# Another written order of the steps in a hybrid attention and gMLP block

## The chip, the cores and the metric

The kernel runs on one core of a Trainium2 chip. The metric is the device time of one execution in microseconds. Engines are named as in the profile: PE is TensorE (matrix products), PEld its weight loads, DVE is VectorE, ACT is ScalarE, POOL is GpSimd, and SP is the queue that issues most transfers.

## The reference

One encoder block on x of 1024 tokens by 1024 channels. One input projection feeds an attention branch, a gated spatial branch, and merge gates:

```python
h = rmsnorm(x, norm_gain)
z = jnp.einsum('bsd,de->bse', h, w_in)
q, k, v, gate_a, u_in, v_in, gate_b, g_merge = jnp.split(z, IN_SPLITS, axis=-1)
q = axial_rope(rmsnorm(q by head, q_gain), ...)      # 8 heads of 64
k = axial_rope(rmsnorm(k by head, k_gain), ...)      # 2 heads of 64
attn = block_attention(q, k, v) * jax.nn.silu(gate_a)
y_a = attn @ w_proj_attn
u = jax.nn.gelu(u_in)
vv = layernorm(jax.nn.gelu(v_in), ln_v_gain, ln_v_bias)
v_mix = jnp.einsum('gij,bcjgd->bcigd', w_spatial, vv) + b_spatial   # within chunks of 128 tokens
gm = u * v_mix * jax.nn.silu(gate_b)
y_b = gm @ w_proj_gmlp
g = jax.nn.sigmoid(g_merge + b_merge)
y = g[0] * y_a + g[1] * y_b
return rmsnorm(x + y @ w_out, final_gain)
```

## The kernel before

Nearly every matrix product is done as three products of a high and a low part (lines 184 to 187, and likewise elsewhere), so each operand is cast by ScalarE (the high part, line 124 or 286) and subtracted by VectorE (the low part, line 130 or 287). The stages follow each other:

- The k and v projections (tile kv, lines 203 to 227) run over eight slices of 128 channels of x. Each slice is loaded, split into a tile xhl, and used for 48 products. The eight xhl tiles fill the eight buffers of tag "X".
- v_group(0) to v_group(3) (line 458) compute the spatial branch's v input, 48 products each, from the xhl tiles and from weights in tiles nh and nl; the two nl tiles fill the two buffers of tag "ptr". A GELU on ScalarE (line 465) writes each result to a vst tile. v_post (line 368) is the layer norm of one 128-token chunk, and spatial (line 381) mixes positions.
- load_pair, norm_part and norm_split (lines 291 to 315) load x again in four pairs of channel slices (tiles xp), multiply by the rows' norm rB (line 299), and split into f16 tiles x16. The pairs and the two vst tiles share the four buffers of tag "qT". The x16 tiles of slices 4 to 7 lie in tag "X".
- prep_q (line 505) loads, casts and splits one eighth of the q weights. Its raw tile comes from the four buffers "wraw", which also hold the two raw halves of the spatial weights (load_wsp, line 474) until bias_term (line 493) has read them. Its output lies in "ptr".
- q_group (line 529) makes q for 256 tokens, q_norm (425) its head norm and rotary positions, q_split (431) its split and transposes. head_norm and rope (395 and 410) do the same for k (tile kn), split and k_transposes follow.
- The maximum of v (lines 1032 to 1038: the multiplication by the rows' norm, and a reduction to vab) gives a scale for v; lines 1082 to 1097 finish it, beginning with a transpose vabT on TensorE, and vS holds the scaled and split v.
- scores (line 629) handles 128 queries of one head: products, maximum (637), exponential (641), split (647 and 648), and a transposing transfer to a tile T (652). mix2 (654) multiplies T with v for two blocks. run_fill (685) is half of one tile of the u, a or b projections, whose weights come from prep_next; all of them use one PSUM bank, tag "z". v_affine (559) applies the layer norm's gain and bias after the spatial product.
- proj_b, x_chunk, pair_weights, gate, proj_a and square_out (lines 701 to 994) are the output side: projections, merge gates and the preparation of the output weights. The output product and the final norm end the kernel.

From line 998 on, one flat list of calls sets the written order of all this. The compiler doesn't keep it: it forecasts when each instruction is ready, places instructions on the engines by that, and lets the written order decide between those that are ready. A few blocks under tc.high_priority() go ahead of all. Once placed, each engine and each transfer queue executes strictly in its order and waits for the buffers and values that the head of its queue needs. The scales of the weights come from squares (line 334), whose raw tiles are loaded from ScalarE's queue into tag "xa" (line 333).

## Time and profile before

| | |
|---|---|
| three runs | 714.37, 715.13, 716.05 us; median 715.13 |
| the profiled execution | 716.34 us, of which 714.6 us is its span |
| PE, DVE, ACT, POOL busy | 684.1, 576.6, 478.8, 99.8 us |
| instructions | 12246 |
| mean granted clock of TensorE | 0.99 |

In the timelines a row has the start, the busy time, the engine, the line, the operation and its tiles; the brackets hold how long the engine sat idle before it and what it waited for. A row with xN merges N like instructions, and its time then runs from the first one's start to the last one's end. In lists of waits the three figures are the total, the number of times, and the longest.

### The profile page before, as it was taken

Reading aid. Unit: us, or ns where it says so; the run is one execution under the profiler, and the core shown is the slowest. Engines: PE = TensorE matmul, PEld = TensorE weight load, DVE = VectorE, ACT = ScalarE, POOL = GpSimd, SP = SyncE. Lnnn points to the kernel's source line nnn. Section 1 sums busy time; section 2 is a strip of 40 time slices with the busy share of each in tenths; the row PEclk is TensorE's granted clock in tenths of the full one; section 3 lists DMA queues with packets and bytes.
Section 4 is the critical chain, followed back from the end, with each engine's and each line's share of the span. In section 5 each row is a group of like instructions: output and inputs, shape, how many; then the busy total and the mean of one; then the engine's idle time right before and its main releaser. Section 6 shows DMA issues by size and latency. Waiting matters only on the chain.

```text
span 714.6 us, 12246 instructions
## 1 busy us (share of the span) xinstructions
PE 684.1 (96%) x4753; PEld 398.0 (56%) x4753; DVE 576.6 (81%) x831; ACT 478.8 (67%) x890; POOL 99.8 (14%) x114
## 2 busy tenths in 40 slices
PE   8999799998998999999999999999999999999996
PEld 8888545454464555545546885644645564444443
DVE  6577999999898997899788998979879887972233
ACT  6676558976788987789676697585784647831011
POOL 0026043044020011001000022001020102000000
PEclk9999999999999999999999999999999999999998
DMA  8990444634679997799997730440520043410202
GB/s 298 402 403 9 162 156 152 210 59 90 118 167 169 198 202 131 149 223 178 175 187 169 228 104 1 143 152 0 202 78 16 1 165 128 179 53 36 118 30 89
DMA packets 159818, 102.40 MB, mean 143 GB/s; under 512 B 136208, under 2 KB 136848, under 8 KB 159760
## 3 DMA queue, kind: packets, MB, share of 16 engines
q1 hardware_dynamic: 158320, 97.14, 52.8%
q10 hardware_dynamic: 1440, 4.47, 1.6%
q8 instruction: 37, 0.61, 0.3%
q14 instruction: 21, 0.17, 0.1%
HBM read 63.85 MB, written 4.19 MB: 95 GB/s over the span
## 4 chain that ended last, share of the span: by engine, by line
PE 48%; DVE 18%; DMA 12%; ACT 11%; issue 5%; POOL 4%; SPq 1%; POOLq 0%; ACTq 0%; DVEq 0%
PE out L187 4%; PE out L186 4%; PE out L185 4%; DMA T<-p 3%; DVE p L648 3%; DMA wraw<-in_wall_dram 3%; PE g L187 3%; PE g L185 3%; DMA xraw<-in_xT_dram 3%; PE g L186 3%; DVE nm L637 2%; PE o L662 2%; ACT P L641 2%; ACT p L647 2%; DMA xn<-in_x_dram 1%
## 5 line engine op out<-in xcount | busy, mean ns | idle before, releaser
L648 DVE SCALAR_TENSOR_TENSOR p<-P,ri,p 128x1024 f16<-128x1024 f32 x64 | 83.4, 1309 | 12.2 <-ACT p L647 11.8
L641 ACT ACTIVATE P<-s,nm 128x1024 f32<-128x1024 f32 x64 | 71.1, 1111 | 29.0 <-DVE nm L637 18.9
L637 DVE TENSOR_REDUCE nm<-s 128x1 f32<-128x1024 f32 x64 | 77.5, 1215 | 1.9 <-PE s L635 1.8
L647 ACT ACTIVATE p<-P,ri 128x1024 f16<-128x1024 f32 x64 | 72.7, 1140 | 3.6 <-DVE ri L644 1.9
L662 PEld LDWEIGHTS <-vS 128*64 128x64 f16 x1536 | 45.9, 111 | 19.2 <-issue 16.6
L662 PE MATMUL o<-T,vS 128*64 128x128 f16 x1536 | 51.2, 222 | 5.5 <-DMA T<-p 5.4
L634 PE MATMUL s<-kT,qT 128*128 128x512 f16 x128 | 49.2, 384 | 2.2 <-ACT P L641 2.2
L186 PE MATMUL out<-wo,yhl 128*128 128x512 f16 (+2 forms) x136 | 49.5, 366 | 0.0
L187 PE MATMUL out<-wo,yhl 128*128 128x512 f16 (+2 forms) x136 | 49.3, 366 | 0.0
L185 PE MATMUL out<-wo,yhl 128*128 128x512 f16 (+2 forms) x136 | 49.0, 366 | 0.0
L635 PE MATMUL s<-kT,qT 128*128 128x512 f16 x128 | 48.9, 382 | 0.0
L953 ACT ACTIVATE sq<-xr 128x1024 f32<-128x1024 f32 x7 | 7.4, 1059 | 58.8 <-DVE xr L1374 58.4
L1374 DVE SCALAR_TENSOR_TENSOR xr<-out,osc,xr 128x1024 f32<-128x1024 f32 x7 | 9.0, 1284 | 40.7 <-PE out L187 40.7
L185 PE MATMUL g<-x,wg 128*128 128x512 f16 x96 | 36.5, 380 | 0.0
L187 PE MATMUL g<-x,wg 128*128 128x512 f16 x96 | 36.4, 379 | 0.1
L186 PE MATMUL g<-x,wg 128*128 128x512 f16 x96 | 36.4, 379 | 0.0
L279 POOL TENSOR_SCALAR scg<-scg 128x1 f32<-128x1 f32 x8 | 2.0, 250 | 197.7 <-ACT usg L278 197.7
L186 PE MATMUL q<-wq,x 128*128 128x512 f16 x64 | 24.7, 388 | 2.7 <-DVE wq L287 2.7
L185 PE MATMUL q<-wq,x 128*128 128x512 f16 x64 | 24.8, 388 | 0.5 <-ACT wq L286 0.5
L186 PE MATMUL v<-nl,xhl 128*128 128x512 f32 x64 | 25.2, 393 | 0.0
L186 PE MATMUL yb<-gm,wh 128*128 128x512 f32 x64 | 25.2, 393 | 0.0
L185 PE MATMUL v<-nh,xhl 128*128 128x512 f32 x64 | 25.1, 392 | 0.0
(571 smaller groups left out, 1925.9 us busy)
## 6 DMA issues: line engine op xcount, KB each, us to landing
wraw<-in_wall_dram SPq DMA_DIRECT2D x91, 256.0 KB, 3.2
graw<-in_wall_dram SPq DMA_DIRECT2D x16, 512.0 KB, 4.7
xraw<-in_xT_dram SPq DMA_DIRECT2D x13, 512.0 KB, 5.6
xn<-in_x_dram SPq DMA_DIRECT2D x8, 512.0 KB, 8.2
xp<-in_xT_dram SPq DMA_DIRECT2D x8, 512.0 KB, 6.3
wor<-in_wall_dram SPq DMA_DIRECT2D x8, 512.0 KB, 5.2
xr<-in_x_dram SPq DMA_DIRECT2D x8, 512.0 KB, 3.8
out_dram<-xr SPq DMA_DIRECT2D x7, 512.0 KB, 2.6
```

The source lines that it names most:

```text
L185: pe.matmul(o, ah, bh, start=start, stop=False)
L186: pe.matmul(o, ah, bl, start=False, stop=False)
L187: pe.matmul(o, al, bh, start=False, stop=stop)
L634: pe.matmul(sp[:, H(hf)], qs, kT[v][:, 0, H(hf)], start=True, stop=False)
L635: pe.matmul(sp[:, H(hf)], qs, kT[v][:, 1, H(hf)], start=False, stop=True)
L637: dve.tensor_reduce(out=nm, in_=sp, axis=AX.X, op=ALU.max, negate=True)
L641: act.activation(Pt, sp, AF.Exp, bias=nm, accum_out=rsum)
L647: act.activation(hi, Pt, AF.Copy, scale=ri)
L648: dve.scalar_tensor_tensor(out=lo, in0=Pt, scalar=ri, in1=hi, op0=ALU.mult, op1=ALU.subtract)
L662: pe.matmul(ot[64 * h:64 * h + 64, C(k)], vS[:, kt, v, 64 * vl:64 * vl + 64], T[:, h, 8 * p + kt, :], start=(n == 0), stop=(n == len(parts ...
L953: act.activation(sq, xn, AF.Square, accum_out=rs)
L1374: dve.scalar_tensor_tensor(out=xr[tt], in0=sps[tt], scalar=osc[:, 4:5], in1=xr[tt], op0=ALU.mult, op1=ALU.add)
```

## The change

The list of calls is written in another order. No call is added or removed, and no function is changed. In the part up to the scores:

```diff
+    early = scales(["q"] + order[:4], ["xa"] * 8)
+    v_group(0)
     bsp = t2("bsp")
...
     Ak, Bk = (heads(t) for t in tabk)
-    early = scales(["q"] + order[:4], ["xa"] * 8)
-    v_group(0)
+    load_pair(0)
+    rB = t4("rB", "rB")
...
+    v_group(1)
+    load_pair(1)
+    with tc.high_priority():
+        scales_end(*early)
...
     load_wsp(0)
+    load_wsp(1)
+    v_group(2)
+    load_pair(2)
+    prep_q(0)
+    v_post(0)
+    norm_part(3)
+    load_pair(3)
+    norm_part(2)
+    ktmp = t4("vS", "ktmp")
+    head_norm(kn, ktmp, 0, 8, "kf")
+    norm_part(0)
+    prep_q(1)
+    scale_wsp()
+    norm_part(1)
+    prep_q(2)
+    v_group(3)
     v3 = vn.rearrange("p (t e) -> p t e", e=128)
...
-    v_post(0)
-    rB = t4("rB", "rB")
...
-    load_wsp(1)
-    scale_wsp()
-    v_group(1)
-    ktmp = t4("vS", "ktmp")
-    head_norm(kn, ktmp, 0, 8, "kf")
-    load_pair(1)
-    load_pair(0)
-    v_group(2)
...
-    v_post(1)
-    prep_q(0)
-    prep_q(1)
-    load_pair(2)
-    norm_part(4)
-    load_pair(3)
-    rope(kn, ktmp, Ak, Bk, 8, 2)
-    norm_split(4)
-    v_group(3)
-    prep_q(2)
     bias_term(0)
     prep_q(3)
+    v_post(1)
+    norm_part(7)
     prep_q(4)
-    norm_part(1)
+    norm_part(5)
+    norm_part(4)
     prep_q(5)
...
+    rope(kn, ktmp, Ak, Bk, 8, 2)
     v_post(6)
...
+    prep_q(6)
+    norm_split(4)
...
+    spatial(0)
+    norm_split(3)
+    v_post(3)
+    v_post(2)
+    norm_split(0)
+    norm_split(7)
+    prep_q(7)
...
+    k_transposes(0)
+    norm_split(1)
+    norm_split(6)
     k_transposes(1)
+    norm_split(5)
+    norm_split(2)
     k_transposes(2)
+    bias_term(1)
+    q_group(0)
+    q_norm(0)
```

In the attention some thirty calls change places by a few positions: q_norm(2) moves from before the first scores to behind the fifth, q_norm(3) from behind the fifth to behind the seventh, v_affine(0) from behind the twenty-third scores to behind the twelfth, and mix2, run_fill, prep_next and scores are interleaved differently. In the output side:

```diff
+    x_chunk(0)
...
     load_chunk(1)
-    pws[0] = pair_weights(0)
-    x_chunk(0)
     proj_b(0)
+    load_chunk(2)
     proj_b(1)
     proj_b(2)
+    pws[0] = pair_weights(0)
     proj_b(3)
+    proj_b(4)
+    load_chunk(3)
+    proj_b(5)
     x_chunk(1)
-    load_chunk(2)
-    proj_b(4)
     x_chunk(2)
-    load_chunk(3)
     x_chunk(3)
     make_forms(gat, 2, g_tile, GA, ASUB, AHI, ALO)
-    proj_b(5)
     proj_b(6)
...
-    pws[4] = pair_weights(4)
-    gate(4)
     square_out(4)
     square_out(3)
+    pws[4] = pair_weights(4)
     pws[5] = pair_weights(5)
+    gate(4)
```

## The prediction

> **What bounds the kernel now.** I read the page first, then the busy time by stages, then the waits of TensorE, then the timelines of all queues between 40 and 92 us. The page:

> ```profile
> PE 684.1 (96%) x4753; PEld 398.0 (56%) x4753; DVE 576.6 (81%) x831; ACT 478.8 (67%) x890; POOL 99.8 (14%) x114
> ```

> TensorE is busy for 684.1 of 714.6 us, and no operation is added or removed. So the new order can only win or lose in the remaining 30.5 us, and in stretches at a reduced clock. By stages (columns: length, busy time and instructions of PE, PEld, DVE, ACT, POOL, then clock, DMA share, GB/s):

> ```profile
> 0.00:40.00 40.00, 36.57 (x250) 33.92 (x251) 21.83 (x45) 27.89 (x46) 3.21 (x10) 1.00 0.95 355
> 40.00:81.40 41.40, 41.29 (x237) 34.27 (x236) 35.49 (x54) 26.86 (x47) 14.81 (x13) 1.00 0.49 188
> 81.40:90.50 9.10, 3.81 (x17) 1.37 (x16) 9.10 (x13) 5.79 (x8) 0.00 (x0) 0.96 0.26 86
> 90.50:141.40 50.90, 49.33 (x366) 25.09 (x366) 46.41 (x84) 40.99 (x83) 15.76 (x18) 0.97 0.56 176
> 141.40:380.00 238.60, 226.63 (x2209) 121.43 (x2208) 213.68 (x278) 192.02 (x347) 38.22 (x30) 0.99 0.84 155
> 380.00:445.00 65.00, 63.84 (x449) 47.48 (x447) 59.84 (x88) 50.89 (x92) 7.67 (x4) 1.00 0.49 134
> ```

> The densest loss is 81.4 to 90.5, at the start of the q projection: TensorE works 3.81 of 9.10 us while VectorE is full. The attention (141.4 to 380) loses 238.6 - 226.63 = 12.0 us spread out, and VectorE is idle for only 24.9 us there. I call the 81.4 stretch stall A. Its instructions on TensorE, with the idle time before each in brackets:

> ```profile
> 78.94 1.03 PE L497 MATMUL wsum<-wspr,ones 128*128 128x256 f32 x4
> ...
> 82.06 0.38 PE L186 MATMUL q<-wq,x 128*128 128x512 f16 x1 [0.32 <-DVE wq L287]
> ...
> 83.86 0.38 PE L186 MATMUL q<-wq,x 128*128 128x512 f16 x1 [0.34 <-DVE wq L287]
> ...
> 85.61 0.38 PE L185 MATMUL q<-wq,x 128*128 128x512 f16 x1 [0.51 <-ACT wq L286]
> 88.06 0.30 PE L1085 MATMUL vabT<-identr,vscr 128*128 128x128 f32 x1 [2.07 <-DVE bsp L499]
> 90.41 0.59 PE L186 MATMUL q<-wq,x 128*128 128x512 f16 x1 [2.05 <-DVE wq L287]
> ```

> Idle in A: 0.32 + 0.34 + 0.51 + 2.07 + 2.05 = 5.29 us. All but the 2.07 us (the transpose vabT waits for its PSUM bank, which VectorE's bias term holds) is for the cast or the split of a q weight. The two largest other waits of TensorE in all are these:

> ```profile
> PE o L662 <- DMA T<-p: 5.4, 5, 2.5
> PE ga L568 <- DVE uw L590: 3.4, 1, 3.4
> ```

> An idle time also costs what comes after it. The stretches of 5 us (length, PE busy, clock, DMA share, GB/s) in which these waits end, beside a shorter wait that ends before 130:

> ```profile
> 85.00:90.00 5.00, 0.78 (x3) 0.97 0.15 50
> 90.00:95.00 5.00, 4.59 (x16) 0.69 0.50 158
> 125.00:130.00 5.00, 3.43 (x52) 1.00 0.66 189
> 130.00:135.00 5.00, 5.00 (x42) 1.00 0.74 235
> 160.00:165.00 5.00, 1.64 (x9) 0.98 0.36 67
> 165.00:170.00 5.00, 5.00 (x18) 0.68 0.32 62
> 220.00:225.00 5.00, 3.56 (x17) 1.00 1.33 171
> 225.00:230.00 5.00, 3.98 (x51) 0.66 0.90 184
> ```

> After A, after the wait for uw (stall B) and after the longest wait for T (stall C, 2.5 us) the granted clock falls; after 5.00 - 3.43 = 1.57 us of idling it does not. After A the loss is 5 x (1 - 0.97) + 5 x (1 - 0.69) = 1.7 us; after B (0.98, 0.68) and C (1.00, 0.66) it is again 1.7 each. So A costs 5.29 + 1.7 = 7.0 us, B 3.4 + 1.7 = 5.1, C 2.5 + 1.7 = 4.2. [...]

> **Why A is there.** In step with ScalarE and the transfers:

> ```profile
> 61.30 4.27 ACT L286 ACTIVATE x<-xp,gs 128x1024 f16<-128x1024 f32 x4 [1.06 <-DVE xp L299]
> ...
> 68.25 1.27 ACT L465 ACTIVATE vst<-v,rstd 128x512 f32<-128x512 f32 x2 [2.44 <-PE v L187]
> 76.61 1.15 ACT L286 ACTIVATE x<-xp,gs 128x1024 f16<-128x1024 f32 x1 [7.09 <-DVE xp L299]
> ...
> 78.60 1.33 ACT L286 ACTIVATE wq<-wraw,s0q 128x512 f16<-128x512 f32 x2
> ```

> ```profile
> 40.41 33.26 SPq L294 DMA_DIRECT2D xp<-in_xT_dram  x8
> 82.04 2.13 SPq L134 DMA_DIRECT2D wraw<-in_wall_dram  x3
> ```

> ScalarE idles for 7.09 us at 69.5. Next in its queue is the fifth x split, of pair 2 of the xp tiles, and behind it the first q weights. Pairs 2 and 3 share four "qT" buffers with pairs 0 and 1 and two vst tiles, so their loads (the last four of the eight, issued up to 40.41 + 33.26 = 73.67) wait until VectorE has split pairs 0 and 1. The third and later q weights are queued on SP behind those loads and are issued at 82.04. VectorE meanwhile:

> ```profile
> 45.77 1.22 DVE L1033 TENSOR_TENSOR vn<-vn,rstd 128x1024 f32<-128x1024 f32 x1
> ...
> 48.68 1.99 DVE L1037 TENSOR_REDUCE vscr<-vn 128x128 f32<-128x1024 f32 x1
> ...
> 64.01 0.17 DVE L404 TENSOR_TENSOR kf<-kf,rstd 128x16 f32<-128x16 f32 x1 [2.80 <-POOL kf L146]
> ...
> 65.48 1.43 DVE L419 TENSOR_TENSOR ktmp<-kn,tabk 128x256 f32<-128x256 f32 x4
> 66.83 1.27 DVE L287 SCALAR_TENSOR_TENSOR x<-xp,gs,x 128x1024 f16<-128x1024 f32 x1
> 68.03 1.22 DVE L422 TENSOR_TENSOR kn<-kn,tabk 128x1024 f32<-128x1024 f32 x1
> 69.16 3.68 DVE L287 SCALAR_TENSOR_TENSOR x<-xp,gs,x 128x1024 f16<-128x1024 f32 x3
> 72.77 1.21 DVE L423 TENSOR_TENSOR kn<-kn,ktmp 128x1024 f32<-128x1024 f32 x1
> ```

> The low halves of pairs 0 and 1 (66.83, and three from 69.16) stand behind the maximum of v (L1033 and L1037, 1.22 + 1.99 = 3.2 us), the norm of k with its 2.80 us wait, and part of the rope of k (1.43 + 1.22).

> **The change, part by part.** The written order is not the executed one: the compiler places instructions by its own forecast of when they are ready, and the written order decides between ready ones. Priorities are what changes.

> 1. Maximum of v behind v_group(3), rope of k behind prep_q(5), load_pair(0) and rB directly behind v_group(0), norm_part of dt 3, 2, 0, 1 ahead of the others. 3.2 us (v) and 1.43 + 1.22 = 2.65 us (rope ahead of the last three splits) no longer outrank pairs 0 and 1: 5.9 us at most, with the 2.80 us wait untouched. The weights cannot follow all the way: the first wq tile shares the two "ptr" buffers with the v weights, which v_group(3) reads. That group begins at 68.25 (ScalarE's wait for v ends there) and ends near 78.94 with the next matmul, so its first half, and with it the buffer, is done at (68.25 + 78.94) / 2 = 73.6, against 78.60 when wq is cast now: 5.0 us. The lower end is 0, if the pair loads move not at all. I take **4.0 us**, nearer to the upper row since 5.9 is offered and 5.0 can be used. A falls to 5.29 - 4.0 = 1.3 us, under the 1.57 that cost no clock, so the 1.7 goes too: **-5.7 us** (ends: 0 and -7.0).

> The 2.80 us wait hangs on the power on GpSimd:

> ```profile
> 56.02 7.95 POOL L146 TENSOR_TENSOR kf<-kf,mhalf 128x16 f32<-128x16 f32 x1 [1.41 <-DVE kf L145]
> ...
> 111.93 3.35 POOL L146 TENSOR_TENSOR qf<-qf,mhalf 128x16 f32<-128x16 f32 x1 [9.71 <-DVE qf L145]
> ```

> The same power takes 7.95 us for k and 3.35 for q. [...]

> 2. What is put off comes due later: 3.2 us of v and 1.43 + 1.22 + 1.21 = 3.9 of rope, 7.1 us in all, into 90.5 to 141.4, where VectorE is idle for 50.9 - 46.41 = 4.5 us. 7.1 - 4.5 = 2.6 us has no room. It costs TensorE nothing if it passes on into the attention's 24.9 idle us, and 2.6 if the first scores wait for it. I take half, **+1.3 us**.

> 3. Early squares ahead, load_wsp behind load_pair, scale_wsp later: the spatial weights are used only after 78.94, and the loads waited for at 40 to 80 us cost TensorE 41.40 - 41.29 = 0.1 us. **0**; without that cover the 7.09 us of ScalarE would grow by a load's time, which part 1's lower end holds.

> 4. q_norm(2) and (3) behind more scores, bias_term(1) earlier, some thirty places of scores, mix2, run_fill, prep_next and v_affine changed: the same 213.7 us of VectorE and 226.6 of TensorE. B could vanish (-5.1: VectorE was finishing q_norm(2) when B waited), or one more like it appear (+5.1). **0**.

> 5. Projections: x_chunk(1) to (3) behind proj_b(5), weights of the pairs elsewhere. TensorE loses 65.0 - 63.84 = 1.2 us from 380 to 445; the eight proj_b cover the chunks' VectorE work. **0**; bounds -1.2, and with the cover gone what VectorE has idle there, 65.0 - 59.84 = +5.2.

> Sum: -5.7 + 1.3 = -4.4 us. The profiled execution took 716.34 us (span 714.6 and 1.7 around it), which gives 711.9; it is 1.2 above the median, 715.13, which is what I forecast against: 715.1 - 4.4 = **710.7**.

> **The rivals.** (a) *The maximum of v lands in the hole.* If pairs 2 and 3 come as late as now, L1033 and L1037 move from 46-51 us, where TensorE didn't need VectorE, into 81.4-90.5, where VectorE has no idle time at all, ahead of the weight splits. A stays and grows by 3.2: 718.3. It decides as soon as the pair loads come less than 3.2 us earlier. For it: the 2.80 us wait for the power of k stays in the queue ahead of the splits. Against: ScalarE has 7.09 us idle to give. (b) *Given back, or not done.* The planner places nearly the same instructions, or the attention, where VectorE is idle for 10% only, eats the 4.4: 715.1. For it: the executed order already ignores the written one (the table of stage 141.4 has both engines full); against: A lies ahead of the attention and TensorE sums to the whole. (c) *A and one of the later stalls go:* with B, 710.7 - 5.1 = 705.6; with C, 706.5; for it the later q_norm(2), against it that the transposes to T are as many.

> **How the numbers follow.** Forecast 0.48, (c) 0.14, (b) 0.15, (a) 0.23. What a measurement can't tell from none is 0.2%, 1.4 us: 713.7 to 716.5. The forecast spans 707 to 714, (c) 701 to 707, (a) 716.5 to 723. Faster: nearly all of 0.48 and (c), 0.60; within: (b) and edges, 0.15; slower: 0.25. The range leaves a tenth out at each end, 703.5 to 719.5; the forecast's own is 707 to 714.

> **What would show it.** Right: the last xp loads issued before 70 us, ScalarE's fifth x split near 72 and first wq near 74, no clock dip around 90, wq waits of TensorE under 1.5 us. Part 2 shows as waits of the first scores or qtp on VectorE. Wrong: xp again issued past 71, or TensorE waiting for vab, or new waits over 2 us between 141 and 380 that add up to 4 or more.

## The result

The changed kernel took 709.16 us in the median (708.01 to 712.45, 7 runs) beside 714.37 us before on the same chip: ratio 0.9931, 95% interval 0.9911 to 0.9952. In a later comparison, beside 715.06 us, it took 709.43 us: 0.9939 (0.9916 to 0.9963). So it is faster by about 4.9 us in the first comparison and 4.4 in the later one; forecast was 4.4 us less than before, 710.7 us. The sum was nearly right. Most of its steps weren't, as the traces show.

The page of the changed kernel, whose profiled execution took 710.94 us (span 709.1):

```profile
PE 682.2 (96%) x4753; PEld 398.6 (56%) x4753; DVE 575.3 (81%) x831; ACT 479.9 (68%) x890; POOL 101.2 (14%) x114
```

The busy time by stages after, with the columns of the table before (length, busy time and instructions of PE, PEld, DVE, ACT, POOL, then clock, DMA share, GB/s):

```profile
81.40:90.50 9.10, 5.92 (x34) 2.54 (x29) 9.10 (x17) 3.49 (x5) 1.57 (x4) 1.00 0.34 110
...
141.40:380.00 238.60, 227.60 (x2291) 123.85 (x2290) 212.30 (x278) 192.31 (x347) 38.20 (x30) 0.99 0.86 156
380.00:445.00 65.00, 65.00 (x375) 46.94 (x374) 62.02 (x90) 49.24 (x90) 14.45 (x8) 1.00 0.43 126
```

Stall A is smaller but still there: TensorE works 5.92 us of the 9.10 instead of 3.81, and VectorE is still full. The attention's stage loses 11.0 us instead of 12.0. From 380 to 445 the 1.2 us of idling is gone. The waits of TensorE after:

```profile
PE o L662 <- DMA T<-p: 5.3, 6, 2.1
PE ga L568 <- DVE uw L590: 3.4, 1, 3.4
PE q L186 <- DVE wq L287: 2.9, 2, 2.1
...
PE vabT L1083 <- DVE bsp L499: 1.1, 1, 1.1
```

Stall B (uw) is unchanged, C is 2.1 us instead of 2.5. The waits for wq are 2.9 us in all.

**What moved in the front.** First five rows of the timeline before that the prediction did not show: the spatial weights' scale on TensorE, and on VectorE their two splits, the last instruction ahead of the 2.80 us wait, and the first split of a q weight.

```profile
49.43 0.28 PE L483 MATMUL uswsp<-wss,mscale 128*128 128x2 f32 x2
55.11 0.75 DVE L287 SCALAR_TENSOR_TENSOR wsw<-wspr,scwsp,wsw 128x512 f16<-128x512 f32 x1
...
55.85 0.75 DVE L287 SCALAR_TENSOR_TENSOR wsw<-wspr,scwsp,wsw 128x512 f16<-128x512 f32 x1
...
59.99 1.22 DVE L299 TENSOR_TENSOR xp<-xp,rB 128x1024 f32<-128x1024 f32 x1
...
81.26 0.75 DVE L287 SCALAR_TENSOR_TENSOR wq<-wraw,s0q,wq 128x512 f16<-128x512 f32 x1
```

Now the timeline after, in this order: SP, GpSimd, TensorE, ScalarE, VectorE.

```profile
40.62 28.43 SPq L294 DMA_DIRECT2D xp<-in_xT_dram  x8
79.62 14.92 SPq L134 DMA_DIRECT2D wraw<-in_wall_dram  x8
...
54.94 3.82 POOL L146 TENSOR_TENSOR kf<-kf,mhalf 128x16 f32<-128x16 f32 x1 [0.75 <-DVE kf L145]
...
67.10 0.28 PE L483 MATMUL uswsp<-wss,mscale 128*128 128x2 f32 x2
...
72.51 1.15 ACT L286 ACTIVATE x<-xp,gs 128x1024 f16<-128x1024 f32 x1 [0.83 <-DVE xp L299]
...
74.50 1.33 ACT L286 ACTIVATE wq<-wraw,s0q 128x512 f16<-128x512 f32 x2
...
48.91 2.00 DVE L1068 TENSOR_REDUCE vscr<-vn 128x128 f32<-128x1024 f32 x1
...
54.77 1.22 DVE L299 TENSOR_TENSOR xp<-xp,rB 128x1024 f32<-128x1024 f32 x1
...
57.14 2.35 DVE L299 TENSOR_TENSOR xp<-xp,rB 128x1024 f32<-128x1024 f32 x2
59.41 0.16 DVE L404 TENSOR_TENSOR kf<-kf,rstd 128x16 f32<-128x16 f32 x1
...
60.87 1.43 DVE L419 TENSOR_TENSOR ktmp<-kn,tabk 128x256 f32<-128x256 f32 x4
62.21 2.48 DVE L287 SCALAR_TENSOR_TENSOR x<-xp,gs,x 128x1024 f16<-128x1024 f32 x2
64.60 1.22 DVE L422 TENSOR_TENSOR kn<-kn,tabk 128x1024 f32<-128x1024 f32 x1
...
72.33 0.74 DVE L287 SCALAR_TENSOR_TENSOR wsw<-wspr,scwsp,wsw 128x512 f16<-128x512 f32 x1
...
78.85 0.75 DVE L287 SCALAR_TENSOR_TENSOR wq<-wraw,s0q,wq 128x512 f16<-128x512 f32 x1
```

The reduction of v's maximum stands at 48.91 us (before 48.68), and the rope of k still surrounds the low halves of pairs 0 and 1 as before. The planner left both where they were. What moved is the scale of the spatial weights: its products on TensorE from 49.43 to 67.10 us, and with them the two splits on VectorE from 55.11 to 72.33 us. The power of k on GpSimd now takes 3.82 us instead of 7.95, VectorE no longer waits 2.80 us for it, and L404 starts at 59.41 us instead of 64.01. The last loads of xp are issued by 40.62 + 28.43 = 69.05 us instead of 73.67. ScalarE's fifth x split and first q weights come 4.1 us earlier (72.51 for 76.61, 74.50 for 78.60). The third q weight's load gains only 82.04 - 79.62 = 2.4 us. In both kernels this load does not wait for the pair loads but for a raw buffer, which is free when VectorE has split the first q weight (81.26 + 0.75 = 82.01 before, 78.85 + 0.75 = 79.60 after). That split comes 2.4 us earlier and not 4.1, because the two splits of the spatial weights now stand ahead of it.

**What moved in the output side.** Four rows of the timeline before, then three after; wg0T is the first weight of a merge gate's second form, and TensorE waited for it three times between 442 and 445 us.

```profile
425.09 6.56 POOL L280 TENSOR_TENSOR scg<-scg,mhalf 128x1 f32<-128x1 f32 x1
...
431.68 0.72 ACT L286 ACTIVATE wg<-graw,scg 128x512 f16<-128x512 f32 x1 [2.57 <-POOL scg L280]
...
436.50 0.39 PE L185 MATMUL g<-x,wg 128*128 128x512 f16 x1
...
441.50 0.71 ACT L286 ACTIVATE wg0T<-s,scg 128x512 f16<-128x512 f32 x1
```

```profile
424.84 0.73 ACT L286 ACTIVATE wg<-graw,scg 128x512 f16<-128x512 f32 x1
...
432.79 0.39 PE L185 MATMUL g<-x,wg 128*128 128x512 f16 x1
...
436.00 0.71 ACT L286 ACTIVATE wg0T<-s,scg 128x512 f16<-128x512 f32 x1
```

Before, ScalarE stood idle for 2.57 us for the scale scg, and everything it did behind came late. One of the four steps of this scale on GpSimd, a power, took 6.56 us. After, the same power takes 0.94 us, and all four steps together even take longer (12.0 us beside 7.9), but they start 8.8 us earlier, at 415.57 instead of 424.36, and this cast needs no wait. The gates' first product starts at 436.50 us before and at 432.79 after; wg0T's cast comes 5.0 us behind it before and 3.2 us behind it after, and the three waits are gone. It is the same in all profiles here: in the five with the old output order ScalarE waits 2.57 to 2.85 us for scg and TensorE two or three times for wg0T; in the nine with the new order neither waits. The stretch from 442 to 445 us, in which they lay, before and then after:

```profile
442.00:445.00 3.00, 1.86 (x7) 0.54 (x8) 3.00 (x5) 3.00 (x7) 0.00 (x0) 1.00 0.01 3
```

```profile
442.00:445.00 3.00, 3.00 (x15) 1.37 (x14) 3.00 (x6) 1.44 (x2) 0.10 (x1) 1.00 0.00 0
```

### The profile page after: what moved, and what is told of

Same layout as the page of the kernel before. It is cut to its first block, busy times and chain, and to the rows that moved or that the text cites. A ratio compares the mean times of both kernels' runs of the same rounds, so it can differ in the third digit from the quotient of the medians.

```text
span 709.1 us, 12240 instructions
## 1 busy us (share of the span) xinstructions
PE 682.2 (96%) x4753; PEld 398.6 (56%) x4753; DVE 575.3 (81%) x831; ACT 479.9 (68%) x890; POOL 101.2 (14%) x114
## 4 chain that ended last, share of the span: by engine, by line
PE 62%; DVE 13%; DMA 10%; ACT 7%; issue 4%; POOL 2%; SPq 0%; POOLq 0%; ACTq 0%; DVEq 0%
DMA wraw<-in_wall_dram 5%; PE out L186 4%; PE out L187 4%; PE out L185 4%; PE o L662 4%; DVE p L648 3%; PE g L187 3%; PE g L185 3%; PE g L186 3%; DVE nm L637 3%; DMA T<-p 3%; PE yb L186 2%; PE yb L185 2%; PE yb L187 2%; ACT p L647 2%
## 5 line engine op out<-in xcount | busy, mean ns | idle before, releaser
L662 PEld LDWEIGHTS <-vS 128*64 128x64 f16 x1536 | 46.9, 113 | 18.1 <-issue 17.0
L662 PE MATMUL o<-T,vS 128*64 128x128 f16 x1536 | 51.9, 224 | 5.3 <-DMA T<-p 5.3
L186 PE MATMUL out<-wo,yhl 128*128 128x512 f16 (+2 forms) x136 | 49.5, 366 | 0.0
L187 PE MATMUL out<-wo,yhl 128*128 128x512 f16 (+2 forms) x136 | 49.3, 366 | 0.0
L185 PE MATMUL out<-wo,yhl 128*128 128x512 f16 (+2 forms) x136 | 49.0, 366 | 0.0
L185 PE MATMUL g<-x,wg 128*128 128x512 f16 x96 | 36.5, 380 | 0.0
L187 PE MATMUL g<-x,wg 128*128 128x512 f16 x96 | 36.4, 379 | 0.1
L186 PE MATMUL g<-x,wg 128*128 128x512 f16 x96 | 36.4, 379 | 0.0
L279 POOL TENSOR_SCALAR scg<-scg 128x1 f32<-128x1 f32 x8 | 5.3, 666 | 191.3 <-ACT usg L278 191.3
L186 PE MATMUL q<-wq,x 128*128 128x512 f16 x64 | 24.1, 379 | 2.9 <-DVE wq L287 2.9
L185 PE MATMUL yb<-gm,wh 128*128 128x512 f32 x64 | 25.2, 394 | 0.0
L185 PE MATMUL v<-nh,xhl 128*128 128x512 f32 x64 | 25.2, 393 | 0.0
L186 PE MATMUL yb<-gm,wh 128*128 128x512 f32 x64 | 25.1, 393 | 0.0
L186 PE MATMUL v<-nl,xhl 128*128 128x512 f32 x64 | 25.1, 392 | 0.0
```

The costliest lines, as they stand in the source:

```text
L185: pe.matmul(o, ah, bh, start=start, stop=False)
L186: pe.matmul(o, ah, bl, start=False, stop=False)
L187: pe.matmul(o, al, bh, start=False, stop=stop)
L662: pe.matmul(ot[64 * h:64 * h + 64, C(k)], vS[:, kt, v, 64 * vl:64 * vl + 64], T[:, h, 8 * p + kt, :], start=(n == 0), stop=(n == len(parts ...
```

## The experiments

Twelve runs. The first questions were which part of the change carries the gain, and through what; three runs tried to take away what was left of A and B.

### The one call that moved

The traces show how little of the new front reached the engines. The changed kernel and the run below, in which one call of the front is moved and nothing else, execute the same instructions in the same order: on GpSimd to the end, on TensorE up to the 1345th product (206.5 us, in the attention), on VectorE, ScalarE and SP beyond that. So the front was tried by that call:

```diff
     load_wsp(1)
-    scale_wsp()
     v_group(1)
...
     prep_q(1)
+    scale_wsp()
     load_pair(2)
```

> The kernel before with one call moved: scale_wsp() (scale and split of the spatial weights) from behind load_wsp(1) to behind prep_q(1). Theory 1, that the part up to the scores gains because these two splits leave VectorE's queue ahead of the splits of pairs 0 and 1, and the power of k is then no longer waited for: the last four xp loads are issued near 67 us instead of 71.7, TensorE keeps its full clock at 90 us, scores begin 2.9 us earlier, and the time falls by 2.9 us or a little more. Theory 2 (the prediction's step 1), that the order of v's maximum, the rope of k and the norm parts gives it: the loads stay near 71.7 us and the time stays within 1 us of before.

Measured: 712.70 us beside 715.22, ratio 0.9971 (0.9956 to 0.9987). Its timeline has the short power and no wait behind it:

```profile
54.73 3.81 POOL L146 TENSOR_TENSOR kf<-kf,mhalf 128x16 f32<-128x16 f32 x1 [0.74 <-DVE kf L145]
...
59.20 0.16 DVE L404 TENSOR_TENSOR kf<-kf,rstd 128x16 f32<-128x16 f32 x1
...
84.81 0.30 PE L1085 MATMUL vabT<-identr,vscr 128*128 128x128 f32 x1 [0.48 <-DVE bsp L499]
87.16 0.59 PE L186 MATMUL q<-wq,x 128*128 128x512 f16 x1 [2.06 <-DVE wq L287]
...
148.62 0.38 PE L634 MATMUL s<-kT,qT 128*128 128x512 f16 x1 [1.32 <-ACT P L641]
```

Of the idling before and in the q projection two waits are left, 0.48 + 2.06 = 2.54 us for 5.29. The call is the front's whole change, and it pays: 0.29%, 2.1 us, somewhat less than the 2.9 expected, and the clock at 90 us was not kept (0.50 from 87.01 to 90.42 us). A part comes back at once: the first scores of the attention wait 1.32 us for ScalarE.

### The three parts in every combination

Attention only takes the new calls from the first scores to gm_split; output only the new order from mix2 of the last block on. Of the output's diff, the beginning:

```diff
-    pws[0] = pair_weights(0)
-    x_chunk(0)
     proj_b(0)
+    load_chunk(2)
     proj_b(1)
     proj_b(2)
+    pws[0] = pair_weights(0)
     proj_b(3)
+    proj_b(4)
+    load_chunk(3)
+    proj_b(5)
     x_chunk(1)
```

> The kernel before with the new order of the attention alone (from the first scores to the last but one mix2, with q_norm(2) behind the fifth scores); the part up to the scores and the output side are those of before. If the parts add up as the two traces say, the first yb product comes 0.8 us earlier and the time falls by about 0.8 us. If the attention hands a gain through unchanged and gives nothing of its own: within 0.5 us of before.

> The kernel before with the new order of the output side alone (from gm_split(2) on). If the parts add up: the three waits of TensorE at 442 to 444 us go, and the time falls by 1.2 to 1.7 us. The prediction's step 5: 0. If the output side only gained because the attention ended earlier: 0 as well, with the waits still there.

> The kernel before with the new order of attention and output side, and the old one up to the scores. If the parts add up: 0.8 + 1.7 = 2.5 us less than before, and the rest of the change, 2.9 us, is what the first part gives. If the parts hinge on each other: far from e2 and e3 together.

> The kernel before with the moved call of scale_wsp() and with the new order of the output side; the attention keeps its order. If the parts add up, the call brings its share (the run with the call alone stood at 0.9971 of before, about -2.1 us) and the output side its own (0.998, about -1.4 us): 0.995, about -3.5 us, and what is then missing to the whole change (0.9931) is the attention's. If the whole gain needs the attention's order to keep what the call won (the call alone gave 1.3 to 1.7 us back at the attention's start), this kernel stays at about 0.997.

> The kernel before with the moved call of scale_wsp() and with the new order of the attention; the output side keeps its order. If the parts add up: 0.9971 x 0.9995 = 0.9966, about -2.4 us. If the new attention order keeps what the call won and the call alone gave back: about 0.9950, -3.5 us, and then the output side's -1.4 completes the whole change's -4.9.

> The changed kernel again, beside the two kernels with two parts each, on one chip: 0.9931 as before, between 0.991 and 0.996. Its profile is the second one of this kernel: if the front's gain is steady, the first score product comes again near 138.4 us (before: 141.3), the power of k takes 3.8 us, and the three waits of TensorE at 442 to 444 us are absent.

| call | attention | output | ratio to before | 95% interval |
|---|---|---|---|---|
| x | | | 0.9971 | 0.9956 to 0.9987 |
| | x | | 0.9995 | 0.9977 to 1.0014 |
| | | x | 0.9980 | 0.9962 to 0.9998 |
| | x | x | 0.9975 | 0.9955 to 0.9995 |
| x | | x | 0.9939 | 0.9921 to 0.9956 |
| x | x | | 0.9968 | 0.9944 to 0.9992 |
| x | x | x | 0.9931 and 0.9939 | 0.9911 to 0.9952, 0.9916 to 0.9963 |

Each part can be taken as the mean of four differences, with 0.9935 for the whole: the call 0.29, 0.27, 0.41 and 0.40%, in the mean 0.34% or 2.4 us; the output side 0.20, 0.20, 0.32 and 0.33%, in the mean 0.26% or 1.9 us; the attention 0.05, 0.05, 0.03 and 0.04%, 0.3 us, each less than its interval. Within the intervals the parts add up (alone 0.29 + 0.05 + 0.20 = 0.54%, together 0.65%). The call and the output side together, without the attention's thirty moved calls, cannot be told from the whole. Which of the moved calls of the output side brings its gain was not taken apart. That the new attention order is needed to keep what the call won was one of the theories on record; 0.9939 against it settles that it isn't.

The profile of the output side alone, in the 3 us of the three waits:

```profile
442.00:445.00 3.00, 3.00 (x16) 1.35 (x15) 3.00 (x5) 0.96 (x2) 0.00 (x0) 1.00 0.02 5
```

The three kernels here with the old front have the long power of k, 7.95 us in each.

### Is it the two splits on VectorE?

The call moves products, scales on GpSimd, casts on ScalarE, and splits on VectorE. Here only VectorE's two splits, with a small product lgs, come behind the rope of k, once in the old kernel and once in the one with both late parts new. The products, the scale and ScalarE's casts stay early (the casts at 53.21 us in the first, 53.47 in the second; before, 53.59), although the second expectation counts the casts among what moves:

```diff
+    def split_wsp(sc):
...
-    scale_wsp()
+    scw = scale_wsp()
...
-    rope(kn, ktmp, Ak, Bk, 8, 2)
+    kdone = rope(kn, ktmp, Ak, Bk, 8, 2)
+    with tc.issue_after(kdone.ins):
+        split_wsp(scw)
```

> The kernel before, with the scale of the spatial weights computed as early as there (product, GpSimd steps and casts), and only VectorE's two low halves and the small product lgs ordered behind the rope of k. It tells apart why GpSimd's power for k took 7.95 us in before, e2, e3 and e4, and 3.81 us in after and e1. If VectorE's spatial splits alone make the difference: the power takes about 3.8 us, VectorE doesn't wait at L404, the last xp loads go out near 67 us, and the scores begin 3 to 4.7 us earlier. If the scale's own steps on GpSimd or the tight sequence of two-input instructions do it: the power takes near 8 us again, and the loads come 1.5 us earlier at most.

> The kernel before with the new order of attention and output side, as in the run with both late parts (0.9975), and in the front, in place of the moved call, only the two VectorE splits of the spatial weights and their casts on ScalarE behind the rope of k; the scale of the spatial weights and its two products on TensorE stay early. If the way by VectorE (the two splits leave the queue ahead of the norm of k, the power of k takes 3.8 us for 7.95, the loads of pairs 2 and 3 go 4.6 us earlier) is what carries the gain of the front, the time is that of the whole change: 0.993 to 0.9945, about 710.5 us. If something else that the moved call shifts carries it (the place of the two products on TensorE, or what the planner makes of the queues behind them), it stays at 0.9975 or above, about 713 us or more, as the same splits without the new late parts did (1.0003).

Measured: 714.59 us, ratio 1.0003 (0.9987 to 1.0019), and in the new surroundings 712.25 us, 0.9968 (0.9948 to 0.9987), where both late parts without it stood at 0.9975. In the profile of the first the products are as early as before, at 48.88 us, the power is short, and the last four xp loads go out from 67.26 us and the first scores start at 138.08, as expected:

```profile
48.88 0.28 PE L483 MATMUL uswsp<-wss,mscale 128*128 128x2 f32 x2
...
54.97 3.82 POOL L146 TENSOR_TENSOR kf<-kf,mhalf 128x16 f32<-128x16 f32 x1 [0.74 <-DVE kf L145]
```

So it is shown that the place of the two splits in VectorE's queue makes the power of k long (7.95 us in the kernel before, 3.82 in both trials), and VectorE's 2.80 us wait for it. That this carries the time of the call is not shown: the same way was taken twice and brought 0.03% of loss and 0.07% of gain, neither of which can be told from nothing. The second stands between the two theories on record, 0.9945 or less and 0.9975 or more. The stretch from 81.4 to 141.4 us says how far the splits go. The three fences are the kernel before, the one call, and the splits late in the old kernel:

```profile
81.40:141.40 60.00, 53.13 (x382) 26.47 (x381) 55.51 (x96) 46.78 (x91) 15.76 (x18) 0.97 0.51 162
```

```profile
81.40:141.40 60.00, 57.46 (x407) 28.91 (x406) 55.76 (x97) 47.43 (x93) 19.09 (x18) 0.97 0.51 162
```

```profile
81.40:141.40 60.00, 55.92 (x397) 27.88 (x395) 55.64 (x96) 47.14 (x90) 17.16 (x18) 0.97 0.52 167
```

TensorE idles for 6.9, 2.5 and 4.1 us, each with one half-clock period (0.97), 1.7 us more. Idling and 1.7 us for each such period together are 7.1 to 8.6 us in the four profiles with the old front, 5.8 and 6.0 in the two with the splits late, and 3.8 to 5.3 in five with the moved call. So in this stretch the splits late give some 2.2 us of the call's 3.6, and the time of the whole shows nothing of them. Each of these profiles is one execution, and that of the splits late in the old kernel was the fastest of its ten (713.12 us, median 714.59), so it flatters them.

The trial is also not as clean as its edit. The planner placed more than the splits anew: against the kernel before, TensorE's order differs in 64 products, up to 201 us, and with the one call in 10. On VectorE a multiplication by rB and an x split now stand ahead of the first q weight (from 77.55 to 79.89 us), and so the third q weight's load, for which that split makes room, is issued at 80.66 and 81.13 us in the two trials, at 78.79 to 79.62 in five profiles with the moved call, and at 81.05 to 82.04 in the four with the old front. This fits the times, but it was not tried by itself. What the two splits alone are worth, and what else the call does, stays open.

### Three tries at what is left

All three start from the changed kernel. The first reads the spatial sums early, so that vabT does not wait; the second puts the eviction of uw, for which B waits, on ScalarE; the third does both.

```diff
+    with tc.high_priority():
+        bias_term(0)
+        bias_term(1)
```

```diff
-        dve.tensor_scalar(out=w, in0=zp, scalar1=sc, scalar2=None, op0=ALU.mult)
+        act.activation(w, zp, AF.Copy, scale=sc)
```

> The changed kernel with bias_term(0) and (1) written directly behind load_wsp(1), ahead in priority. This frees the PSUM bank that vabT waits for. If the first wait of what is left of stall A (1.1 us, vabT for the bank) is only that bank: it goes, TensorE reaches the scores about 1.1 us earlier, time -1. If VectorE's late q weights hold TensorE anyway, the wait moves to the q product behind it: 0. The raw spatial tiles are still held until the splits, so the q weight loads come no earlier than in after.

> The changed kernel with the eviction of the u product's bank (uw) moved from VectorE to ScalarE, to take stall B away: 3.35 us of idling and, by the clock, 1.7 us after it. If B costs what the prediction's price says and nothing takes its place: -5 us. If ScalarE is as late there, or the following scores wait instead: between 0 and -2 us.

> e6 and e7 together. If the stalls are separate: the sum of the two, up to -6 us against the changed kernel, near 703.5 us beside a kernel before of 715. If the attention gives back what comes earlier: no better than the better of the two.

Measured, as ratios to the kernel before: 1.0096 (1.0072 to 1.0119), 1.0017 (1.0001 to 1.0033) and 1.0168 (1.0140 to 1.0196). All lose what the change had won and more, and none did what was expected of it. The waits of TensorE with the early sums, and then with the eviction on ScalarE:

```profile
PE sp L389 <- ACT vhl L124: 5.5, 1, 5.5
```

```profile
PE ga L568 <- ACT uw L590: 2.6, 1, 2.6
PE s L634 <- ACT P L641: 2.2, 2, 1.8
PE u L568 <- ACT uw L590: 2.1, 2, 1.5
```

In the first the wait for vabT is gone, but the planner then put four of the spatial products between those of the q projection, at 104.29 us, where they wait 5.5 us for ScalarE. In the second B shrinks by 0.8 us, and ScalarE, which now owes TensorE one thing more, is waited for by the scores (2.2 us, 1.3 in the changed kernel) and by u (2.1 us). That B comes from an eviction in a full VectorE queue is neither shown nor refuted by this; the remedy costs more than B.

## Why the prediction was right and wrong

**The signs** named for being right came true in the first profile, all but one: loads before 70 us, the fifth split near 72, the first weights near 74, no fall of the clock around 90, but not waits for wq under 1.5 us. They test the shift and not what makes it; the cause was another.

**The place** was half right. The stretch around stall A gains, as forecast; the other gain, nearly as large, lies in the output side, where the forecast had none.

**Step 1 failed in its cause.** It said that the maximum of v (3.2 us) and part of the rope (2.65 us) would no longer outrank pairs 0 and 1. Both run where they ran: the written order had been moved for them, the placed order was not. What moved is what step 3 had listed as "scale_wsp later" and costed at 0. That step asked whether TensorE waits for the spatial weights; it did not ask what stands behind their two splits on VectorE, which is the norm of k, the power on GpSimd, and its 2.80 us wait. The prediction had the row of that wait and called it untouched.

**Its size was closer.** The pair loads came 4.6 us earlier for the 4.0 taken, the fifth x split 4.1. But the shift does not arrive whole. The prediction had the third and later q weights held up by the pair loads in SP's queue; what they wait for is the raw buffer that VectorE's first q split frees, and this comes only 2.4 us earlier, behind the moved splits. A shrank from 5.29 to 1.12 + 2.05 + 0.87 = 4.04 us (1.05 + 2.06 = 3.11 in the second profile), not to 1.3. The sum over the four pairs of kernels gives the call 2.4 us where step 1 had 5.7 and step 2 gave 1.3 back, 4.4 net. The waits for wq that were to fall under 1.5 us are 2.9.

**The 1.7 us for the clock** rested on a wrong estimate. The prediction took it that a wait of 1.57 us costs no clock and one of 2.07 does. In the first profile of the changed kernel, with waits of 1.12, 2.05 and 0.87 us, A costs no clock (1.00 from 83.02 to 93.26 us); in its second profile, where TensorE waits 1.05 and 2.06 us there, it does (0.50 from 87.25 to 90.66). The last section has the rows.

**Step 2**, 1.3 us given back to the first scores: not by its way, since nothing of v or rope was put off. The one call does give back 1.32 us there, to a wait for ScalarE; in the two profiles of the changed kernel this wait is absent and 0.71 us.

**Step 4**, 0 for the attention: right, 0.3 us and not told from none.

**Step 5**, 0 with a bound of -1.2: the term that was mis-sized. It measured -1.9 us. The cover was judged by VectorE's load; the engine that was late was ScalarE, through a 2.57 us wait for a scale that pair_weights makes. The bound of 1.2 us was the idling inside 380 to 445, and that went entirely. From the first product of proj_b to the first of proj_a it takes 66.9 to 67.5 us in every profile with the old output order and 65.5 to 65.8 in every one with the new.

So the sum of -4.4 met -4.9 by luck: a front that was sized too high by 2.0 us met an output side that was sized too low by 1.9.

**The rivals.** (a), the maximum of v in the hole, did not come about, since it did not move. (b), that the planner places nearly the same, is true of the front and the attention to a degree that the prediction did not expect (the attention's new order alone moves 104 of TensorE's 4753 products), and wrong for the one call and the output side. (c) needs B or C to vanish: B is 3.4 us as before.

## What to carry to other kernels

Where a planner places the instructions, compare placed orders before costing an edit: of a front of some hundred moved lines one call had an effect. When a step moves, ask of each of its instructions what stands behind it in its queue, also when its own result isn't waited for; this is the question that step 3 left out. And an earlier input is worth only as much as the next thing that comes late lets through: here 4.6 us at the pair loads, 4.1 at ScalarE, 2.4 at the weight loads, and 2.4 in time.

## What the runs showed of the hardware

```profile
86.28:89.69 3.41, 0.30 (x1) 0.16 (x2) 3.41 (x7) 1.44 (x2) 0.00 (x0) 1.00 0.00 2
89.69:93.10 3.41, 2.69 (x7) 1.01 (x7) 3.41 (x10) 0.00 (x0) 1.75 (x4) 0.50 0.44 126
...
127.24:130.65 3.41, 1.87 (x46) 1.65 (x47) 3.38 (x7) 2.58 (x6) 0.00 (x0) 1.00 0.76 223
```

The changed kernel, at A:

```profile
83.02:86.43 3.41, 1.79 (x8) 0.65 (x7) 3.41 (x7) 2.46 (x4) 0.00 (x0) 1.00 0.18 60
86.43:89.84 3.41, 1.85 (x9) 0.87 (x9) 3.41 (x9) 0.00 (x0) 0.91 (x3) 1.00 0.19 58
89.84:93.26 3.42, 2.55 (x16) 1.20 (x14) 3.42 (x8) 1.92 (x3) 1.97 (x4) 1.00 0.52 174
```

The changed kernel's second profile, at A:

```profile
83.83:87.25 3.42, 0.76 (x4) 0.16 (x2) 3.42 (x7) 2.24 (x3) 0.00 (x0) 1.00 0.02 6
87.25:90.66 3.41, 2.96 (x8) 1.00 (x8) 3.41 (x10) 0.15 (x1) 1.94 (x5) 0.50 0.51 154
```

In the first profile the grid cuts A's two waits apart, each period has over half of its time busy (1.79 and 1.85 of 3.41), and the clock stays. In the second both waits fall into one period with 0.76 us of work, and the next runs at half. Counted over all 14 profiles here, up to 695 us: of periods at full clock in which TensorE was busy for under 44% of the time, 37 of 37 were followed by one at half; between 44 and 55%, 2 of 15; above, none of some 2,700. In the first profiles of the two kernels alone it was 5 of 5, busy for 9 to 39% (the row at 86.28 before, 0.30 of 3.41 us, is the lowest), 0 of 4, busy for 52 to 55%, and none of 390. Once at half, it came back after each of the 39 periods with over 65% of work (in those two profiles 5, with 79 to 100%) and after none of the 7 with less (one of them in the changed kernel's second profile, 2.15 of 3.41 us from 158.93 us). By the clock column a half period costs an estimated 3.41 x 0.5 = 1.7 us of dense work. The length of the waits alone doesn't decide it: A loses the clock or keeps it with waits of about 1 and 2.05 us.

**The power of k takes 3.8 or 7.95 us**, the same in every profile of one order, though its instruction never changes: 7.95 in the four profiles with the two splits of the spatial weights around its start, 3.82 in the ten others. In all fourteen it ends 2.76 or 2.77 us after the end of a multiplication by rB (L299) on VectorE. In the ten this is the one under way when the power starts: after the change it ends at 54.77 + 1.22 = 55.99 us, and the power at 54.94 + 3.82 = 58.76. In the four it is the last one, behind which VectorE runs dry: before, 59.99 + 1.22 = 61.21, and the power 56.02 + 7.95 = 63.97. That the power first waits for this multiplication and then takes 2.77 us is the author's estimate from these ends; no run tried it. It can't be so for every such multiplication: after the change VectorE runs two more from 57.14 us on, while the power is at work until 58.76. Why the power's end goes with the first such multiplication in one order, and in the other only with the last of the three behind the second split (56.52, 58.25 and 59.99 us before), is open.
